# Third weight sum on VectorE, the FFN inputs in another order and other buffers, and the down projection's residual added by DMA

## Chip, core and metric

The kernel runs on one NeuronCore of a Trainium2 chip. The metric is the device time of one execution in microseconds (us): 2263.05 us before the change, the median of three runs (2258.35 to 2268.36). Times inside the execution come from one profiled run of 2262.26 us, whose span from the first to the last instruction is 2260.6 us. TensorE's matmul queue is PE, VectorE is DVE, ScalarE is ACT, GpSimd is POOL and SyncE's DMA queue is SP.

## What is computed

One layer of a hybrid decoder runs over 512 prompt tokens and 8 sample tokens, 520 columns in all. Everything is in 32-bit floats, and the kernel keeps activations transposed: features on the partitions, tokens along the row.

```python
def mixer(xn, ...):
    proj = xn @ w_in                                  # 2048 x 6160
    ...
    out = jnp.concatenate([ya, yb], axis=-1) @ w_out  # 2048 x 2048
    return out, conv_new, s_new

def conv_ffn(xn, prev, w_up, conv_w, conv_b, w_down):
    u, v = jnp.split(xn @ w_up, 2, axis=-1)           # 2048 x 11264
    cu, new = causal_dwconv(u, prev, conv_w)
    h = jax.nn.silu(cu + conv_b) * v
    return h @ w_down, new                            # 5632 x 2048

def trunk(x, ...):
    m, c_new, s_new = mixer(rmsnorm(x, norm_mix_g[l]), ...)
    x = x + m
    f, f_new = conv_ffn(rmsnorm(x, norm_ffn_g[l]), ...)
    x = x + f
    return rmsnorm(x, final_norm_g), ...
```

## The kernel before

**Stages.** The kernel runs the input projection with the gated convolution and the linear attention (to 683 us), the mixer's output projection `wo` (683 to 880 us), the up projection with the convolution gate (880 to 1778 us), the down projection (1778 to about 2190 us) and the end with the final norm. Every matmul is a 128x128 weight tile against 260 columns. A product of full precision takes three of them: weights and activations are split into a rounded part (`hi`, `xh`) and the rest (`lo`, `xl`), and hi·xh, hi·xl and lo·xh are summed.

**Seven products.** The last three projections multiply 2x2 block matrices by seven block products instead of eight (Winograd's form of Strassen's scheme). The seven products of a group run in the order `ORDER` = 1, 5, 6, 2, 7, 3, 4; each has 24 matmuls. Their weights are four blocks, `raw[1,1]`, `raw[1,2]`, `raw[2,1]`, `raw[2,2]`, of 128x1024 numbers (512 KB each), and sums of them: a tile `s` holds first raw[2,2]+raw[2,1] (product 5), then that plus raw[1,1] (product 6), then that plus raw[1,2] (product 3), and raw[2,1] takes raw[1,1] on top (product 7). `weights` (L1016) loads the blocks and says who forms each sum: VectorE by an entry of `sums`, or an accumulating DMA of GpSimd by an entry of `dma`. The third sum is a DMA in the second chunk of `wo` (`dma3`) and VectorE's elsewhere; the seventh is VectorE's in the very first group and a DMA in all others.

**Groups.** `wo` has two chunks `c` of the contraction with four groups `g` each, `up` has 44 groups, `down` five chunks of four groups. The main loop (L1403 to L1479) walks through all products `i`. At product 0 of a group it issues three of the next group's weight loads (`begin`), at product 2 the fourth (`load_rest`), and two products ahead `prepare` makes `hi` on ACT and `lo` on DVE and forms the next sum. After each call `in_order` ties the instructions of every engine and of both DMA queues to the order of the program, so an instruction that waits holds up all that follow on its engine or queue.

**Results of wo and down.** `chunk_finish` (L1256) copies the partial sums in PSUM to other banks (ACT, L1269) and adds the finished ones onto `acc[g, q]`, four SBUF tiles of 128x520 per group (DVE, `onto`, L1263). `load_residual` (L1216) fills these tiles with the residual by POOL's queue before the first chunk adds to them: x for `wo`, and x1 (x plus the mixer's result) for `down`.

**Inputs of the FFN.** In the second chunk of `wo`, `projected(g)` (L1302) turns `acc` into the inputs of the up projection, in steps numbered by products since the group's first one; a step of 7 or more falls into the next group. `ready(q)` stores `acc[g, q]` to DRAM as x1 (L1308, SP) and scales it into `xg[q]` (ACT, L1311). `square(q)` squares `acc` on ACT into a tile `fh` and adds that by DMA (POOL) to the norm's sum `ssq`, whose second half is the tile `R`. `sub`, `minus` and `split` form the seven inputs, "forms" 1 to 7. Forms 2 and 3 are written over the `acc` tiles. Forms 5, 4 and 6 have no home yet in the first three groups: `out` splits them into a fresh tile and the source and stores both to `t_d` in DRAM (L1331, SP), and `load_sum` (L1367) loads them back during the last group. Fresh tiles come from `tmp()`, a rotation of eight 128x520 tiles named `t`; a tile is given out again when all that reads it is done, a store to DRAM included.

**The gate.** `gate(t)` (L1148) multiplies the up projection's two halves `z` and `v` by `R`, runs the convolution and forms h. For t < 2 the factor `R` comes late, and z is multiplied as a whole there.

## Time and profile before

| | |
|---|---|
| median of three runs | 2263.05 us (2258.35 to 2268.36) |
| profiled execution | 2262.26 us |
| its span | 2260.6 us |
| mean granted TensorE clock | 0.986 of 2.4 GHz |
| busy ACT, POOL | 1039.6 us (46%), 461.4 us (20%) |
| DMA | 419.10 MB, mean 185 GB/s |
| chain that ended last | PE 88%, DMA 6%, DVE 3% |

A row of the timeline gives start, duration, engine, line, operation and tiles, and in brackets how long the engine had been idle before it and what ended that. A releaser is the instruction whose end came last among those waited for. Where the granted clock reads below 1.00 over a stretch, TensorE ran at 1.2 GHz for part of it.

### The profile page before, as it was taken

The page shows a single profiled execution, that of the slowest core. Times are in us where ns is not written, and L with a number is a line of the kernel's source. Part 1 is how long each engine was busy: PE and PEld are TensorE (multiplying, and loading weights), DVE is VectorE, ACT ScalarE, POOL GpSimd, SP SyncE. Part 2 cuts the span into 40 slices and gives each one's busy share as a digit, 9 for nine tenths or more (in the row PEclk, how much of TensorE's full clock was granted, in tenths as well). Part 3 has the DMA queues.
Part 4 walks back from the last instruction along what each step waited for, and adds up shares of the span by engine and source line. Part 5 has one row for each costly group of instructions (what it writes and reads, how often), then busy time and mean ns, then how long its engine had stood idle before and what let it go on. Part 6 is the DMA issues. An engine that isn't in the chain of part 4 may idle for free.

```text
span 2260.6 us, 43939 instructions
## 1 busy us (share of the span) xinstructions
PE 2195.8 (97%) x17963; PEld 2172.9 (96%) x17963; DVE 1631.3 (72%) x2188; ACT 1039.6 (46%) x1486; POOL 461.4 (20%) x640
## 2 busy tenths in 40 slices
PE   8999999999999977999999999999999999999997
PEld 7998999999999977999999999999999999999997
DVE  5345364444448676888989889889898777778776
ACT  5334434322334465555555555555555444444445
POOL 3023132221323311121221222113121500000100
PEclk9999999999999989999999999999999999999999
DMA  8343354374787789476676766667666987876944
GB/s 249 84 126 105 107 156 113 87 210 121 201 248 242 219 233 299 126 195 174 167 195 160 194 173 178 183 160 193 174 180 191 308 236 218 258 205 195 282 122 151
DMA packets 459751, 419.10 MB, mean 185 GB/s; under 512 B 21353, under 2 KB 413445, under 8 KB 459405
## 3 DMA queue, kind: packets, MB, share of 16 engines
q1 hardware_dynamic: 418353, 285.89, 43.7%
q0 software_dynamic: 39872, 128.17, 21.7%
q8 instruction: 141, 2.31, 0.4%
q10 hardware_dynamic: 1324, 2.23, 0.3%
q14 instruction: 61, 0.50, 0.1%
HBM read 294.13 MB, written 79.25 MB: 165 GB/s over the span
## 4 chain that ended last, share of the span: by engine, by line
PE 88%; DMA 6%; DVE 3%; ACT 1%; POOL 1%; issue 1%; SPq 0%; ACTq 0%; DVEq 0%; POOLq 0%
PE mm L1108 27%; PE mm L134 25%; PE ms L1108 11%; PE y L1249 8%; PE x L1249 8%; PE f L1249 3%; PE e L1249 3%; PE ms L830 1%; DMA t_d<-t 1%; DMA form<-g_d 1%; DMA x_d<-acc 1%; DVE lo L1087 1%; DMA raw<-in_w_down_dram 0%; DMA acc<-x_d 0%; PE ms L1516 0%
## 5 line engine op out<-in xcount | busy, mean ns | idle before, releaser
L1083 ACT ACTIVATE hi<-raw 128x1024 fp32r<-128x1024 f32 x288 | 304.4, 1057 | 225.7 <-issue 79.5
L1108 PE MATMUL mm<-yh,hi 128*128 128x260 f32 x1408 | 398.6, 283 | 2.8 <-ACT ms L1118 2.4
L1108 PE MATMUL mm<-yl,hi 128*128 128x260 f32 x1408 | 397.8, 283 | 0.0
L1108 PE MATMUL mm<-yh,lo 128*128 128x260 f32 x1408 | 397.5, 282 | 0.0
L1087 DVE TENSOR_TENSOR lo<-raw,hi 128x1024 fp32r<-128x1024 f32 x288 | 351.3, 1220 | 57.7 <-ACT hi L1083 57.6
L1087 DVE TENSOR_TENSOR lo<-s,hi 128x1024 fp32r<-128x1024 f32 x216 | 265.3, 1228 | 111.0 <-ACT hi L1083 105.6
L1083 ACT ACTIVATE hi<-s 128x1024 fp32r<-128x1024 f32 x216 | 228.4, 1057 | 223.9 <-DVE s L1032 92.6
L1108 PEld LDWEIGHTS mm<-yh,hi 128*128 128x128 f32 x1408 | 265.1, 188 | 3.3 <-ACT ms L1118 2.6
L1108 PEld LDWEIGHTS mm<-yl,hi 128*128 128x128 f32 x1408 | 265.9, 189 | 0.0
L1108 PEld LDWEIGHTS mm<-yh,lo 128*128 128x128 f32 x1408 | 265.8, 189 | 0.1
L1108 PE MATMUL ms<-b,hi 128*128 128x260 f32 x1408 | 256.6, 282 | 4.6 <-DVE b L118 4.6
L106 DVE TENSOR_TENSOR lo<-raw,hi 128x1024 fp32r<-128x1024 f32 x112 | 144.4, 1290 | 138.1 <-ACT hi L105 131.5
L105 ACT ACTIVATE hi<-raw 128x1024 fp32r<-128x1024 f32 x112 | 118.0, 1055 | 265.3 <-PE mm L134 226.2
L1108 PEld LDWEIGHTS ms<-b,hi 128*128 128x128 f32 x1408 | 217.1, 188 | 4.8 <-DVE b L118 4.8
L1249 PE MATMUL y<-form,hi 128*128 128x260 f32 x1120 | 210.7, 288 | 11.2 <-ACT f L1269 11.2
L1249 PE MATMUL x<-form,hi 128*128 128x260 f32 x1120 | 208.4, 286 | 9.2 <-ACT f L1269 7.4
L1036 POOL DMA_DIRECT2D raw<-raw x71 | 63.5, 895 | 700.1 <-DVE s L1032 585.2
L1108 PE MATMUL ms<-b,lo 128*128 128x260 f32 x704 | 198.5, 282 | 0.0
L1249 PEld LDWEIGHTS y<-form,hi 128*128 128x128 f32 x1120 | 177.6, 193 | 11.6 <-ACT f L1269 11.6
L1249 PEld LDWEIGHTS x<-form,hi 128*128 128x128 f32 x1120 | 175.5, 191 | 10.0 <-ACT f L1269 7.6
L1032 DVE TENSOR_TENSOR s<-s,raw 128x1024 f32<-128x1024 f32 x140 | 170.9, 1221 | 2.5
L1249 PE MATMUL y<-form,lo 128*128 128x260 f32 x560 | 161.3, 288 | 3.8 <-DVE lo L1087 3.8
(324 smaller groups left out, 5563.1 us busy)
## 6 DMA issues: line engine op xcount, KB each, us to landing
raw<-in_w_up_dram SPq DMA_DIRECT2D x176, 512.0 KB
raw<-in_w_down_dram SPq DMA_DIRECT2D x96, 512.0 KB
raw<-in_w_in_dram SPq DMA_DIRECT2D x92, 512.0 KB
raw<-raw POOLq DMA_DIRECT2D x71, 512.0 KB, 5.9
form<-f_d SPq DMA_DIRECT2D x126, 260.0 KB
f_d<-t POOLq DMA_DIRECT2D x80, 260.0 KB, 5.3
raw<-in_w_out_dram SPq DMA_DIRECT2D x32, 512.0 KB
form<-g_d POOLq DMA_DIRECT2D x56, 260.0 KB, 7.9
```

The costliest lines, as they stand in the source:

```text
L105: nc.scalar.activation(hi, raw, AF.Copy)
L106: nc.vector.tensor_tensor(lo, raw, hi.bitcast(F32), op=ALU.subtract)
L134: nc.tensor.matmul(o, w, xx, start=first and i == 0, stop=last and i == 2)
L830: nc.tensor.matmul(pb[:, c * 64 : (c + 1) * 64], L[:, c, :], rhs[:, c], start=True, stop=True,)
L1032: return lambda: nc.vector.tensor_tensor(out, x, y, op=ALU.add)
L1036: return lambda: nc.gpsimd.dma_start(out, x, accum_op=ALU.add)
L1083: nc.scalar.activation(his[i], src, AF.Copy)
L1087: nc.vector.tensor_tensor(los[i], src, his[i].bitcast(F32), op=ALU.subtract)
L1108: nc.tensor.matmul(st["bank"][b], w[:, k, :], x, start=b not in st["used"] and k == 0 and j == 0, stop=k == 7 and j == 2, skip_group_check ...
L1249: nc.tensor.matmul(ps[:, m, :], w[:, k, m * P : (m + 1) * P], x, start=b not in st["used"] and k == 0 and j == 0, stop=k == 3 and j == 2, ...
```

## The change

Five edits, in the order of the diff:

- **Weight sums.** The third sum is always VectorE's. The seventh is a DMA for `up` and for all chunks but the first of `wo` and `down`; in both first chunks VectorE forms it.
- **Gate.** For t < 2, z is multiplied by R first and v three products later; for other t, v as before.
- **Residual of down.** `load_residual` serves `wo` alone. In `down`, the first chunk writes its first result onto `acc` instead of adding it (ACT, with the sign as scale; four of six), and during the second chunk `add_residual` adds x1 by accumulating DMAs of POOL's queue, four per group, for the group two further on.
- **Stores of x1.** In the last group of `wo`, tiles 1 and 2 of `acc` are copied into a fresh tile (ACT) and stored from there.
- **Order of the FFN's inputs.** Form 2 is split one product earlier, t4 is written over `xg[2]` instead of a fresh tile, form 7 is split half a product later, and form 6 is stored one product later, at 10.5.

```diff
@@ -1013,7 +1013,7 @@
-    def weights(source, dma3):
+    def weights(source, dma7):
@@ -1038,17 +1038,15 @@
         }
-        sums = {5: plus(s, raw[2, 2], raw[2, 1]), 6: plus(s, s, raw[1, 1])}
-        dma = {}
-        if state:
-            dma[7] = dma_plus(raw[2, 1], raw[1, 1])
-        else:
+        sums = {
+            5: plus(s, raw[2, 2], raw[2, 1]), 6: plus(s, s, raw[1, 1]), 3: plus(s, s, raw[1, 2]),
+        }
+        if not dma7:
             sums[7] = plus(raw[2, 1], raw[2, 1], raw[1, 1])
-        if dma3:
-            dma[3] = dma_plus(s, raw[1, 2])
-        else:
-            sums[3] = plus(s, s, raw[1, 2])
-        return dict(src=src, sums=sums, dma=dma, bank={}, used=set(), rest=loads[3])
+        return dict(
+            src=src, sums=sums, bank={}, used=set(), rest=loads[3],
+            seventh=dma_plus(raw[2, 1], raw[1, 1]) if dma7 else lambda: None,
+        )
@@ -1060,7 +1058,8 @@
         kind, at = groups[n]
-        state[kind, at] = weights(source(kind, at), kind == "wo" and at[0] == 1)
+        state[kind, at] = weights(source(kind, at), kind == "up" or at[0] > 0)
@@ -1152,10 +1151,9 @@
         yield d
-        nc.vector.tensor_tensor(v[:, :T], v[:, :T], R, op=ALU.mult)
+        x = z[:, 2 : 2 + T] if t < 2 else v[:, :T]
+        nc.vector.tensor_tensor(x, x, R, op=ALU.mult)
         yield d + 0.5
-        if t < 2:
-            nc.vector.tensor_tensor(z[:, 2 : 2 + T], z[:, 2 : 2 + T], R, op=ALU.mult)
         c = tmp()
@@ -1166,6 +1164,9 @@
         )
+        if t < 2:
+            yield d + 3
+            nc.vector.tensor_tensor(v[:, :T], v[:, :T], R, op=ALU.mult)
         yield d + 3.5
@@ -1213,12 +1214,21 @@
-    def load_residual(kind, g):
+    def new_sums(g):
         for q in range(4):
...
+    def load_residual(g):
+        new_sums(g)
+        for q in range(4):
+            nc.gpsimd.dma_start(two(acc[g, q]), rows_of(xT_d, "wo", g, q))
+    def add_residual(g):
+        for q in range(4):
             nc.gpsimd.dma_start(
-                two(acc[g, q]), rows_of(xT_d if kind == "wo" else x1_d, kind, g, q)
+                two(acc[g, q]), rows_of(x1_d, "down", g, q), accum_op=ALU.add
             )
@@ -1260,7 +1270,11 @@
             a = two(acc[g, q])
-            nc.vector.tensor_tensor(a, a, inner(bk[b]), op=op)
+            if kind == "down" and c == 0 and (q, b) not in ((1, "f"), (3, "a")):
+                scale = 1.0 if op == ALU.add else -1.0
+                nc.scalar.activation(a, inner(bk[b]), AF.Copy, scale=scale)
+            else:
+                nc.vector.tensor_tensor(a, a, inner(bk[b]), op=op)
@@ -1305,7 +1319,12 @@
             a, m = acc[g, q], first_tile("wo", g, q // 2)
-            nc.sync.dma_start(rows_of(x1_d, "wo", g, q), two(a))
+            kept = a
+            if g == NG - 1 and q in (1, 2):
+                kept = tmp()[:, :T]
+                nc.scalar.activation(kept, a, AF.Copy)
+            nc.sync.dma_start(rows_of(x1_d, "wo", g, q), two(kept))
             xg[q] = tmp()[:, :T]
@@ -1347,20 +1366,20 @@
         yield 8
-        t4 = tmp()[:, :T]
+        split(xg[2], *form(2, g))
+        t4 = xg[2]
         minus(t4, t2, xg[2])
...
         out(4, t2)
-        out(7, t4)
         yield 9
         square(1)
-        split(xg[2], *form(2, g))
+        out(7, t4)
+        yield 10
         t3 = xg[1]
         sub(t3, xg[3], xg[1])
-        yield 9.5
-        out(6, t3)
         yield 10.5
         square(2)
+        out(6, t3)
         yield 11
@@ -1396,7 +1415,7 @@
     load_rest(0)
-    load_residual("wo", 0)
+    load_residual(0)
     prepare(0)
@@ -1433,10 +1452,8 @@
         prepare(i + 2)
-        if j == 0 and 3 in state[kind, at]["dma"]:
-            state[kind, at]["dma"][3]()
         if j == 5 and more:
-            state[groups[n + 1]]["dma"][7]()
+            state[groups[n + 1]]["seventh"]()
         run_steps(i + 0.5)
@@ -1448,7 +1465,7 @@
             if c == 0 and j == 4 and g + 1 < NG:
-                load_residual("wo", g + 1)
+                load_residual(g + 1)
             if c == 0 and g == NG - 1 and j >= 1:
@@ -1461,14 +1478,14 @@
                 load_form("down", 0, x)
-            if j == 5:
-                load_residual("down", 0)
         if kind == "down":
...
                 drain()
-            if c == 0 and j == 4 and g + 1 < NG:
-                load_residual("down", g + 1)
+            if c == 0 and j == 0:
+                new_sums(g)
+            if c == 1 and j == 5:
+                add_residual((g + 2) % NG)
             if c + 1 < NCD:
...
                     load_form("down", c + 1, 0)
```

On ACT, this is the stretch of group 2 of `wo`'s second chunk in which the forms of group 1 are written (names: `e`, `f`, `x` PSUM tiles; `hi` the rounded weights; `b` form 2 or 3 in an `acc` tile; `yh` form 7; `t` from `tmp()`). Before:

```order
L1269 ACTIVATE e<-x 128x2x260
L1083 ACTIVATE hi<-raw 128x1024
L117 ACTIVATE t<-t 128x520
L117 ACTIVATE yh_9171<-t 128x520
L1320 ACTIVATE fh<-acc 128x520
L117 ACTIVATE b_9203<-t 128x520
L1083 ACTIVATE hi<-raw 128x1024
L117 ACTIVATE t<-t 128x520
L1269 ACTIVATE f<-x 128x2x260
L1083 ACTIVATE hi<-s 128x1024
```

and of the change, from the same copy of `e` on:

```order
L1283 ACTIVATE e<-x 128x2x260
L117 ACTIVATE b_9158<-t 128x520
L1082 ACTIVATE hi<-raw 128x1024
L117 ACTIVATE t<-t 128x520
L1339 ACTIVATE fh<-acc 128x520
L117 ACTIVATE yh_9200<-t 128x520
L1082 ACTIVATE hi<-raw 128x1024
L1283 ACTIVATE f<-x 128x2x260
L1082 ACTIVATE hi<-s 128x1024
L1339 ACTIVATE fh<-acc 128x520
L117 ACTIVATE t<-t 128x520
```

The second split into `t` (form 6) moved from ahead of the copy of `f` to three instructions behind it, and form 2 (`b_9203`, now `b_9158`) to directly behind the copy of `e`.

On DVE, the changed program has in the same stretch one sum more (`s<-s,raw`, the third):

```order
L118 TENSOR_TENSOR b_9159<-t,b_9158 128x520
L583 SCALAR_TENSOR_TENSOR t<-t 128x520
L1086 TENSOR_TENSOR lo<-raw,hi 128x1024
L118 TENSOR_TENSOR t<-t 128x520
L118 TENSOR_TENSOR yl_9201<-t,yh_9200 128x520
L1032 TENSOR_TENSOR s<-s,raw 128x1024
L1086 TENSOR_TENSOR lo<-raw,hi 128x1024
L1277 TENSOR_TENSOR acc<-acc,y 128x520 x2
```

It stands directly ahead of the `lo` of product 7's weights; before, GpSimd issued a DMA `s<-raw` for it.

On POOL's queue, the changed program's second chunk of `down` reads (each `raw<-raw` is a seventh sum, each `acc<-x_d` a lot of four residual tiles):

```order
L1036 DMA raw<-raw 128x1024 x2
L1230 DMA acc<-x_d 128x2x260 x4
L1036 DMA raw<-raw 128x1024
L1230 DMA acc<-x_d 128x2x260 x4
L1036 DMA raw<-raw 128x1024
L1230 DMA acc<-x_d 128x2x260 x4
L1036 DMA raw<-raw 128x1024
L1230 DMA acc<-x_d 128x2x260 x4
```

The lots of four stood before in the first chunk, as plain loads, with the seventh sums of that chunk between them.

## Rows read from the trace of the kernel before

**Rows 1.** The page's first part: busy time, share, instructions.

```profile
PE 2195.8 (97%) x17963; PEld 2172.9 (96%) x17963; DVE 1631.3 (72%) x2188; ACT 1039.6 (46%) x1486; POOL 461.4 (20%) x640
```

**Rows 2.** PE's timeline, waits between 780 and 940 us and in down.

```profile
782.94 0.80 PE L1249 MATMUL f<-form,hi 128*128 128x260 f32 x2 [3.52 <-ACT hi L1083]
...
838.82 0.80 PE L1249 MATMUL x<-form,hi 128*128 128x260 f32 x2 [7.37 <-ACT f L1269]
...
901.94 0.39 PE L1108 MATMUL ms<-b,hi 128*128 128x260 f32 x1 [4.64 <-DVE b L118]
...
937.85 0.39 PE L1108 MATMUL mm<-yh,hi 128*128 128x260 f32 x1 [2.43 <-ACT ms L1118]
...
1804.37 0.58 PE L1249 MATMUL y<-form,lo 128*128 128x260 f32 x1 [3.81 <-DVE lo L1087]
```

**Rows 3.** Windows: from:to, us; busy PE, PEld, DVE, ACT, POOL; clock; DMA share; GB/s.

```profile
744.59:764.83 20.24, 20.24 (x171) 20.24 (x170) 15.78 (x17) 8.42 (x9) 13.40 (x19) 1.00 0.89 286
764.83:792.24 27.41, 23.43 (x170) 22.92 (x169) 15.06 (x17) 12.58 (x18) 6.37 (x9) 0.88 0.68 195
792.24:819.76 27.52, 22.45 (x171) 22.24 (x170) 20.90 (x27) 17.59 (x28) 4.33 (x6) 0.88 0.87 234
819.76:850.00 30.24, 22.87 (x171) 22.66 (x170) 21.03 (x27) 17.38 (x28) 5.28 (x7) 0.83 0.88 229
850.00:879.92 29.92, 22.29 (x171) 21.90 (x169) 22.36 (x29) 18.34 (x29) 5.68 (x7) 0.89 1.08 307
879.92:907.44 27.52, 22.51 (x173) 22.03 (x173) 17.52 (x22) 12.97 (x21) 2.79 (x4) 0.94 1.12 295
907.44:929.33 21.89, 21.89 (x178) 21.66 (x177) 13.41 (x13) 13.35 (x19) 6.88 (x5) 1.00 0.45 120
929.33:952.30 22.97, 20.54 (x171) 20.26 (x169) 20.97 (x29) 12.79 (x18) 0.86 (x1) 1.00 0.51 127
784.80:892.00 107.20, 87.13 (x650) 86.32 (x650) 81.03 (x100) 68.54 (x111) 17.23 (x20) 0.87 0.93 253
```

**Rows 4.** ACT's timeline: the waits behind the first two of rows 2.

```profile
781.83 1.06 ACT L1083 ACTIVATE hi<-s 128x1024 fp32r<-128x1024 f32 x1 [7.45 <-DMA s<-raw]
...
837.64 0.64 ACT L117 ACTIVATE t<-t 128x520 fp32r<-128x520 f32 x1 [10.08 <-DMA t_d<-t]
```

**Rows 5.** The chain of waits in order of time: start, us, what.

```profile
826.60 11.57 DMA t_d<-t
...
877.18 10.85 DMA x_d<-acc
...
894.03 7.06 DMA x_d<-acc
```

**Rows 6.** DVE's timeline: the waits behind the third and the last of rows 2.

```profile
901.18 0.70 DVE L118 TENSOR_TENSOR b<-t,b 128x520 fp32r<-128x520 f32 x1 [7.74 <-DMA x_d<-acc]
...
1801.96 1.23 DVE L1032 TENSOR_TENSOR s<-raw 128x1024 f32<-128x1024 f32 x1 [6.70 <-DMA raw<-in_w_down_dram]
```

**Rows 7.** Groups of instructions by form, DVE and ACT, 792.24 to 850.00 us.

```profile
L1032 DVE TENSOR_TENSOR s<-s,raw 128x1024 f32<-128x1024 f32 x3 | 3.7, 1225 | 0.1
...
L1263 DVE TENSOR_TENSOR acc<-acc,x 128x520 f32<-128x520 f32 x4 | 2.7, 690 | 0.1
...
L1269 ACT ACTIVATE f<-y 128x520 f32<-128x520 f32 x1 | 0.6, 586 | 0.0
```

**Rows 8.** DMA queues, 1906.9 to 1927.2 us, one group of down: packets, MB, share.

```profile
q1 hardware_dynamic: 2112, 2.10, 33.5%
q0 software_dynamic: 150, 0.55, 14.3%
```

**Rows 9.** Windows of down, columns as in rows 3.

```profile
1778.46:1827.06 48.60, 44.22 (x342) 43.84 (x342) 33.65 (x39) 19.08 (x23) 19.90 (x31) 0.93 1.00 313
1827.06:1867.52 40.46, 40.46 (x338) 40.46 (x337) 31.54 (x33) 16.83 (x18) 2.10 (x3) 1.00 0.79 233
1906.90:1927.20 20.30, 20.30 (x171) 20.30 (x170) 15.86 (x17) 8.41 (x9) 0.86 (x1) 1.00 0.48 131
1947.50:1967.70 20.20, 20.20 (x170) 20.20 (x170) 15.75 (x17) 8.42 (x9) 0.86 (x1) 1.00 1.08 329
```

## The prediction

> **What bounds the kernel now.** I read the page's first part, then the waits of PE in its timeline, then windows over the groups in which they lie, and last the engine or DMA behind each wait. TensorE's matmul queue is busy 97% of the span [rows 1], and the change leaves the number of matmuls alone. So it can give or cost only what PE loses in waits, and in the slow clock behind them.
>
> The losses near the change lie in two places. The first runs from the second chunk of `wo` into the third group of `up`. A group without a wait takes 20.24 us, the first row [rows 3]; the seven that follow take 27.41, 27.52, 30.24, 29.92, 27.52, 21.89 and 22.97 us, together 187.47. Seven times 20.24 is 141.68, and two pairs of small matmuls for the norm add about 1.6. **44.2 us** are lost. The waits of PE make up 31.5 of them: 3.5 for product 3 of the first group, three of one kind (7.37 stands in the rows, 5.07 and 6.10 are its like), 4.64, 2.43, and four small ones of 2.4 together [rows 2]. The other 12.7 us are matmuls at 1.2 GHz behind a wait: the granted clock is 0.83 to 0.89 in the groups of the chunk, 1.00 in the one ahead [rows 3].
>
> The second place is the start of `down`: its first two groups take 48.60 us, the next two 40.46 [rows 9]. Less 0.8 us of marker matmuls and a transpose, **7.3 us** are lost, 3.81 of them in one wait [rows 2].
>
> The causes, wait by wait. (A) Product 3 waits for ACT's `hi<-s`, and that for the third sum by DMA [rows 4]. (B) Three times ACT stands 8 to 10 us before a split into a fresh `t` because the tile's last content is still on its way to `t_d` [rows 4, 5]; the copy of `f`, for which PE waits, stands behind it. PE loses 7.37 us where ACT waits 10.08, so ACT has a lead of 2.7 us. (F) The split of form 3 over `acc` waits 7.74 us on DVE for the store of x1 [rows 5, 6]. (G) The first gates delay a copy of ACT by 2.43 us. (H) In `down`, DVE's sum waits 6.70 us for weights [rows 6] while the DMA engines are full: share 1.00 over the whole stretch [rows 9].
>
> **The change part by part.** Profiled run 2262.26 us, span 2260.6.
>
> *Third sum by VectorE.* (A) goes. DVE pays 1.22 us in each of four groups [rows 7]. It is busy 20.9 us in a group of 20.24 already, by the third row [rows 3], so from the second group on it would be about 1.9 us too long, 5.6 us over three groups; with the lead of 2.7, 2.9 us could reach PE. The busy figure counts overlapping ends of instructions, so nothing may reach it. Bounds 0 and 5.6; I take 1.5, because part runs beside the DMA wait below.
>
> *Seventh sum by VectorE in the first chunks.* Seven more sums at 1.22 us. DVE has 15.8 of 20.2 us to do there [rows 3, 9], so they cost nothing; without that cover it would be 1.22 per group.
>
> *Order and homes of the inputs.* Before, a group takes nine fresh tiles out of a rotation of eight, and form 6 gets the tile from which form 5 was stored two products (5.8 us) earlier; the store spends 11.57 us on the chain alone [rows 5]. Now eight are taken. Form 5's tile is next wanted four products later (11.6 us), form 6's three (8.7 us). With the lead of 2.7 us that covers 11 to 14 us, and form 6's `hi` is now behind the copy of `f`. (B) goes in the first groups. What is late next is the DMA system itself. From 784.8 to 892 us, between the first store of x1 and the last loads of form 6, its share is 0.93: 99.7 us of work, by the last row [rows 3]. The queue of accumulating DMAs worked 14.3% of 20.3 us for one sum [rows 8], 2.9 us; three third sums fall in this stretch, which leaves 91.0 us. Full windows read up to 1.12, the sixth row [rows 3], so that work takes 81 to 91 us. Without waits the first store comes at 778, some 4 us of work are done by 785, and the rest ends between 863 and 872. Product 7 of the first `up` group wants form 6 at 764.8 + 4 x 20.24 + 4 x 2.9 + 1.4 = 859. So 4 to 13 us of wait come back there or just ahead; I take 9. A wait of that size brings slow clock: eight waits brought 12.7 us now, so some 1.6 each, and I add 2.5. Bounds: 0 (sums of squares share these engines and may land later) and 17.
>
> *Copies ahead of the store.* (F) goes for 2 x 0.62 us of ACT, which is busy 13 of 27.5 us there [rows 3]. The split of form 2 comes a product earlier and wants the x1 store of tile 3 in 2.5 products (7.2 us); such a store took 10.85 us at the fullest point [rows 5]. That wait lies ahead of the one for form 6 and inside it, so it adds nothing to the sum.
>
> *Gate.* z first, v later: (G), 2.43 us and its clock, is inside the 44.2.
>
> *Down.* The DMA engines lose before 1800 us two lots of residual (8 x 0.85 us, from 6.8 us for 2.10 MB in rows 8) and one seventh sum, 9.7 us; the late weights were 6.7 late. (H) goes; about 1 us stays of two waits of 0.5 that other things cause. ACT gains 16 copies of 0.586 us in place of DVE's 0.690 [rows 7], 2.3 us per group on 8.4 of 20.3 [rows 9]: nothing.
>
> *Residual added in the second chunk.* Sixteen DMAs; half a sum of 512 KB is 1.5 us, so 5.9 us per lot, 23.5 in all. In the middle groups the engines are half empty (0.48), where chunks meet they are full (1.08) [rows 9], and two of four lots end up there. PE waits nowhere in that stretch, and weights are requested a group ahead. Bounds 0 and 2 x 5.9; I take 0, as in the groups where they are full now and nothing waits.
>
> **Sum.** 44.2 + 7.3 = 51.5 us to be had; 9 + 2.5 + 1.5 + 1 = 14.0 stay. 2262.26 - 37.5 = 2224.8; the median lies 0.8 above the profiled run, so **2225.6 us**.
>
> **Rivals.**
>
> *The wait moves to form 2 (0.20).* With DMA still full in groups two to four, DVE stands before `b` of form 2 until tile 3's x1 has landed: 10.85 against 7.2 us plus the lead of 2.7, 1 to 4 us each, with clock 2 us more, and DVE's own 5.6 us come on top. Some 13 us more stay: 2239. For it: rows 5. Against it: DMA shares of 0.68 to 0.88 in the first three groups, and 2.9 us less work in each.
>
> *All is recovered (0.13).* If DMA takes the 81 us or less, only the 1 us in `down` stays: about 2212.
>
> *The added residual delays weights (0.10).* If the accumulating DMAs are served beside the loads that were asked for earlier, each of two lots at a chunk's end holds them up by 5.9 us, less the lead 3.2, twice, and 1 us of clock: 2233. No wait in [rows 9] shows it; there was no second stream of this size there. The Trainium skill ("DMA: Bandwidth & Descriptors", section "Queues, rings and completion order") says that each DMA engine takes turns between the queues that have work for it, a packet at a time. By that rule the time would be this one; first come, first served would give 2225.6.
>
> *Slower: the DMA engines are the bound (0.04).* If their work, not its order, sets the second chunk's time, the 44.2 us stay under other names, and the 23.5 us of adds come through in full where chunks meet; less 7.3 that is 2279. It decides from a share of 1 in every group of the chunk, and from no slack in weights a group ahead. Against it: 0.68, 0.87 and 0.88 in three groups [rows 3] and 0.48 in `down`. The same page's section "Issuing engines are not separate DMA queues" says that all queues share the same 16 engines. By it the residual costs DMA time wherever it is put; the shares decide whether anyone waits.
>
> That the change doesn't do what it says is no rival: the order of the instructions shows every part.
>
> **Numbers.** Forecast 0.48 (2217 to 2232); the rivals as above; 0.05 for a gain under 0.5%. About 0.5% (11 us) is what a measurement of this kernel can tell from no change. The range runs from all recovered with 3 us for the spread of runs, 2209, to the form 2 case with its upper price and the adds, 2247. Faster 0.90, same 0.06, slower 0.04.
>
> **What would show it.** In the changed profile PE's waits for ACT's copy of `f` are gone, DMA s<-raw is no releaser, and groups one to three of the chunk take 20.2 to 22 us. The fourth, or the first of `up`, is several us too long, with a load from `t_d` or an x1 store behind the wait, at a DMA share above 1. The start of `down` is 6 to 7 us shorter, and no wait on a DMA shows in its second and third chunk. It is wrong if groups of the chunk stay above 25 us, if DVE sets PE's pace there, or if `raw` is waited for where chunks of `down` meet.

## The result, and the profile after

The changed kernel takes **2235.38 us** (median of 4 runs, 2233.18 to 2237.94), the kernel before in the same session 2262.62 us (4 runs, 2258.35 to 2268.36). The ratio is 0.9878, with a 95% interval of 0.9853 to 0.9904. Forecast were 2225.6 us and a range of 2209 to 2247. The sign and the range hold; the time came out 9.8 us longer, and outside the 2217 to 2232 us that had the highest chance (0.48).

The two profiled executions have spans of 2260.6 and 2236.2 us. Their difference of 24.4 us splits at five points of PE's timeline:

| stretch | before | after | difference | forecast |
|---|---|---|---|---|
| start to the first matmul of `wo` (not edited) | 683.35 | 685.43 | +2.1 | 0 |
| second chunk of `wo` and three groups of `up` | 187.47 | 162.55 | -24.9 | -31.2 |
| first two groups of `down` | 48.60 | 41.14 | -7.5 | -6.3 |
| second group of `down`'s third chunk | 20.23 | 24.74 | +4.5 | 0 |
| all else | | | +1.4 | 0 |

PE is busy for 98% of the shorter span (97% in [rows 1]), by the first line of the page:

```profile
PE 2189.3 (98%) x17963; PEld 2165.8 (97%) x17963; DVE 1634.4 (73%) x2183; ACT 1049.2 (47%) x1504; POOL 459.6 (21%) x629
```

The first line of the table is no effect: over fourteen kernels with the same code there it lay between 681.7 and 686.8 us. Inside the second line the chunk's four groups, 27.41, 27.52, 30.24 and 29.92 us in [rows 3], have become shorter; the first group of `up` has grown from 27.52 to 30.97. The windows of the changed kernel by group (us, busy time of PE, PEld, DVE, ACT and POOL, granted clock, DMA share, GB/s), the last the third group of `up`:

```profile
766.91:787.14 20.23, 20.23 (x171) 20.23 (x169) 16.40 (x18) 12.72 (x18) 4.41 (x6) 1.00 0.83 251
787.14:807.83 20.69, 20.46 (x171) 20.28 (x169) 20.62 (x27) 16.23 (x26) 3.39 (x4) 1.00 0.95 269
807.83:829.91 22.08, 20.72 (x170) 20.40 (x169) 21.98 (x28) 17.46 (x29) 3.67 (x6) 1.00 1.05 281
829.91:856.46 26.55, 22.39 (x171) 21.94 (x169) 25.04 (x31) 19.99 (x33) 5.72 (x7) 0.94 1.08 290
856.46:887.43 30.97, 25.78 (x172) 24.44 (x173) 17.96 (x22) 13.71 (x22) 2.54 (x3) 0.83 1.08 298
...
909.34:929.46 20.12, 20.12 (x170) 20.12 (x169) 19.50 (x27) 11.91 (x17) 0.85 (x1) 1.00 0.56 141
```

Against 20.24 us, and 1.6 for the norm's matmuls, 19.3 us are lost where 44.2 were lost before. DVE is busy for 20.62 of 20.69 and 21.98 of 22.08 us in the second and third row, and for 25.04 of 26.55 in the fourth. PE's waits there, from its timeline of the changed kernel (what answers to [rows 2]):

```profile
826.95 0.48 PE L1259 MATMUL x<-form,hi 128*128 128x260 f32 x2 [1.36 <-DVE acc L1277]
850.58 0.48 PE L1259 MATMUL y<-form,hi 128*128 128x260 f32 x2 [2.92 <-DVE acc L1277]
856.46 0.36 PE L1107 MATMUL mm<-bh,hi 128*128 128x260 f32 x1 [1.25 <-DVE acc L1277]
863.89 0.39 PE L1107 MATMUL mm<-yl,hi 128*128 128x260 f32 x1 [0.83 <-DMA yl<-t_d]
865.63 0.38 PE L1107 MATMUL mm<-yh,hi 128*128 128x260 f32 x1 [0.87 <-DMA yh<-t_d]
...
872.46 0.59 PE L1107 MATMUL mm<-yl,hi 128*128 128x260 f32 x1 [2.42 <-DVE yl L118]
```

The waits for ACT's `f`, for `hi<-s` and for the gate are gone. In their place stand waits for DVE's addition to `acc` (it frees the PSUM bank), small ones for loads from `t_d`, and one for DVE's `yl`. DVE makes that `yl` right behind the split of form 2, the step which the change had moved a product earlier, and there it stands 9.21 us for the x1 store, as its timeline and the chain of waits say:

```profile
869.23 0.70 DVE L118 TENSOR_TENSOR b<-t,b 128x520 fp32r<-128x520 f32 x1 [9.21 <-DMA x_d<-acc]
```

```profile
851.40 7.57 DMA t_d<-t
...
858.99 0.02 SPq L1327
...
859.03 10.10 DMA x_d<-acc
```

The chain shows two delays, one behind the other: SP issues the store of x1 only when a store to `t_d` has landed, and the x1 store then needs 10.10 us. SP does not wait for that data. The `t_d` store of 851.40 is the eighth DMA ahead of the x1 store on SP. By the semaphores that the trace records, this program gives SP's DMAs eight in turn (687 of SP's 715 DMAs take the one that the eighth ahead of them had), and each waits until its own is free. The windows of 5 us show the price in clock: 0.50, TensorE's lower level of 1.2 GHz, just behind the waits.

```profile
865.00:870.00 5.00, 3.30 (x13) 2.43 (x13) 0.74 (x2) 2.71 (x5) 0.00 (x0) 0.84 1.06 394
870.00:875.00 5.00, 2.58 (x12) 2.54 (x12) 5.00 (x6) 2.83 (x5) 0.85 (x1) 0.50 1.13 328
```

In `down`, windows by group: the two first groups, then the last of the second chunk and the two first of the third (what answers to [rows 9]):

```profile
1755.63:1776.53 20.90, 20.90 (x173) 20.90 (x174) 16.95 (x21) 12.04 (x17) 6.31 (x12) 1.00 1.08 357
1776.53:1796.77 20.24, 20.24 (x171) 20.24 (x170) 14.39 (x14) 10.49 (x13) 0.00 (x0) 1.00 0.50 155
...
1897.90:1918.12 20.22, 20.22 (x170) 20.22 (x169) 15.78 (x17) 8.41 (x9) 5.76 (x8) 1.00 1.11 282
1918.12:1938.37 20.25, 20.25 (x171) 20.25 (x169) 11.26 (x12) 7.36 (x8) 2.56 (x3) 1.00 1.13 285
1938.37:1963.11 24.74, 20.71 (x170) 20.32 (x169) 20.34 (x21) 9.38 (x10) 1.74 (x2) 1.00 0.85 246
```

The wait at the start is gone. A new one stands where the third chunk has just begun: PE for DVE's `lo`, DVE's sum for `raw`:

```profile
1942.00 0.39 PE L1259 MATMUL y<-form,lo 128*128 128x260 f32 x1 [3.23 <-DVE lo L1086]
```

```profile
1939.59 1.23 DVE L1032 TENSOR_TENSOR s<-raw 128x1024 f32<-128x1024 f32 x1 [6.12 <-DMA raw<-in_w_down_dram]
```

### The profile page after: what moved, and what is told of

Its sections match the earlier page's. It is cut to its first block, busy times and chain, and to the rows that moved or that the text cites. A ratio compares the mean times of both kernels' runs of the same rounds, so it can differ in the third digit from the quotient of the medians.

```text
span 2236.2 us, 43928 instructions
## 1 busy us (share of the span) xinstructions
PE 2189.3 (98%) x17963; PEld 2165.8 (97%) x17963; DVE 1634.4 (73%) x2183; ACT 1049.2 (47%) x1504; POOL 459.6 (21%) x629
## 4 chain that ended last, share of the span: by engine, by line
PE 84%; DMA 2%; DVE 2%; issue 1%; ACT 1%; SPq 0%; ACTq 0%; DVEq 0%
PE mm L1107 28%; PE mm L134 20%; PE ms L1107 11%; PE x L1259 8%; PE y L1259 8%; PE e L1259 3%; PE f L1259 3%; DMA raw<-in_w_down_dram 1%; PE ms L830 1%; DVE lo L1086 0%; DMA t_d<-t 0%; DVE s L1032 0%; DMA x_d<-acc 0%; PE ms L1533 0%; DMA raw<-in_w_out_dram 0%
## 5 line engine op out<-in xcount | busy, mean ns | idle before, releaser
L1036 POOL DMA_DIRECT2D raw<-raw x64 | 57.2, 894 | 651.0 <-DVE s L1032 481.6
L1032 DVE TENSOR_TENSOR s<-s,raw 128x1024 f32<-128x1024 f32 x144 | 176.0, 1222 | 2.5
L134 PE MATMUL mm<-xh,hi 128*128 128x260 f32 x768 | 160.7, 291 | 3.8 <-ACT xh L120 3.8
```

What stands on the lines that cost most here:

```text
L134: nc.tensor.matmul(o, w, xx, start=first and i == 0, stop=last and i == 2)
L1032: return lambda: nc.vector.tensor_tensor(out, x, y, op=ALU.add)
L1036: return lambda: nc.gpsimd.dma_start(out, x, accum_op=ALU.add)
```

## The experiments

Three stretches tell the parts apart in every run: S, the four groups of `wo`'s second chunk and the first three of `up` (where an expectation names a stretch "from the chunk's second group", it is this one, by its numbers); D, the first two groups of `down`; M, the second group of `down`'s third chunk. All from PE's timelines, in us; ratios are to the kernel before on the same chip.

| kernel | S | D | M | median | ratio (95%) |
|---|---|---|---|---|---|
| before | 187.47 | 48.60 | 20.23 | | 1 |
| changed | 162.55 | 41.14 | 24.74 | 2235.38 | 0.9878 (0.9853 to 0.9904) |
| third_alone | 171.30 | 48.61 | 20.23 | 2248.59 | 0.9940 (0.9925 to 0.9955) |
| third_by_dma | 174.58 | 41.14 | 25.46 | 2248.01 | 0.9939 (0.9924 to 0.9954) |
| residual_loaded | 161.08 | 42.61 | 20.23 | 2229.16 | 0.9853 (0.9836 to 0.9870) |
| residual_middle | 159.71 | 41.14 | 20.23 | 2228.95 | 0.9853 (0.9838 to 0.9869) |
| subs_by_pool | 166.49 | 41.14 | 27.02 | 2241.62 | 0.9914 (0.9899 to 0.9929) |
| all_kept | 160.45 | 41.13 | 25.05 | 2234.75 | 0.9880 (0.9863 to 0.9896) |
| store_by_pool | 157.99 | 41.15 | 26.48 | 2233.17 | 0.9874 (0.9859 to 0.9889) |
| down_seventh_dma | 160.29 | 41.14 | 25.16 | 2235.43 (one run) | |
| third_left_out | 158.63 | 41.14 | 25.25 | 2232.38 | 0.9873 (0.9847 to 0.9899) |
| gate_and_copies_undone | 165.04 | 41.14 | 25.54 | 2238.14 | 0.9901 (0.9878 to 0.9923) |
| stores_middle | 158.07 | 41.14 | 20.23 | 2227.53 | 0.9850 (0.9829 to 0.9871) |
| stores_middle_td | 159.25 | 41.14 | 20.23 | 2226.33 | 0.9846 (0.9825 to 0.9868) |

Four kernels have S unedited (changed, residual_loaded, residual_middle, down_seventh_dma): 159.7 to 162.6, mean 160.9. A difference in S of 2 us from one profile is therefore little; the changed kernel's own profile is the slowest of the four.

### third_alone: the kernel before with one edit

```diff
-        state[kind, at] = weights(source(kind, at), kind == "wo" and at[0] == 1)
+        state[kind, at] = weights(source(kind, at), False)
```

> The kernel before with one edit: in the second chunk of wo the third sum is made by DVE instead of an accumulating DMA. Theory (order and homes of the FFN's inputs made most of the gain): PE's wait for hi<-s of product 3 goes (3.5 us and its slow clock, some 5 us together), the waits of ACT for the stores to t_d stay, and DVE, which waits in that chunk anyway, hides its 1.2 us per group. From the chunk's second group to the third group of up about 182 us (187.5 before, 162.6 changed), the whole some 2257 us. Rival (the accumulating DMAs were what filled the DMA engines): the stores come early enough as well, the stretch falls under 170 us, the whole to about 2245.

Measured: S 171.30, 16.2 us less than before, where the theory had some 5 and the rival over 17. The rival is nearly right. ACT's waits for stores to `t_d` did not stay as they were, they became shorter; two of its three, from its timeline, against 10.08 us in [rows 4]:

```profile
826.64 0.64 ACT L117 ACTIVATE t<-t 128x520 fp32r<-128x520 f32 x1 [6.64 <-DMA t_d<-t]
852.19 0.64 ACT L117 ACTIVATE t<-t 128x520 fp32r<-128x520 f32 x1 [5.97 <-DMA t_d<-t]
```

PE's waits for `f` fell with them, from 5.07, 7.37 and 6.10 us to 1.37, 5.20 and 3.55. So the edit helped the stores too, not only product 3. That it did so by taking 512 KB per group off the accumulating queue is the likely reason, but no run isolates it. D is 48.61 as before: this edit does nothing there.

### third_by_dma: the changed kernel without that edit

```diff
+        third = lambda: None
+        if dma3:
+            del sums[3]
+            third = dma_plus(s, raw[1, 2])
...
         prepare(i + 2)
+        if j == 0:
+            state[kind, at]["third"]()
```

> The changed kernel with the third sum of the second chunk of wo given back to an accumulating DMA, all else kept. Theory (DVE too full costs about 4 us there, the DMA engines about as much): PE's wait for hi<-s of some 3.5 us comes back once with its slow clock, three sums of 2.9 us of all DMA engines lengthen the full stretch, DVE's 1.2 us per group go: the stretch takes about 168 us instead of 162.6, the whole some 2241 us (2237 to 2248). Rival (DVE's 21 to 22 us per group are the bound of the second and third group): those groups return to 20.3 us and the whole is no slower than the changed kernel, 2231 to 2236.

Measured: S 174.58, 12.0 us above the changed kernel, twice the theory's 5 to 6. The rival (no slower) is refuted: all four groups of the chunk are 24 to 27.5 us long. The theory let the wait for `hi<-s` come back once, as it stands in [rows 2]. It came back in every group, and one for `lo<-s` behind each:

```profile
781.39 0.80 PE L1264 MATMUL f<-form,hi 128*128 128x260 f32 x2 [2.91 <-ACT hi L1087]
...
805.98 0.51 PE L1264 MATMUL f<-form,hi 128*128 128x260 f32 x2 [0.87 <-ACT hi L1087]
...
831.16 0.51 PE L1264 MATMUL f<-form,hi 128*128 128x260 f32 x2 [2.01 <-ACT hi L1087]
832.42 0.59 PE L1264 MATMUL f<-form,lo 128*128 128x260 f32 x1 [0.75 <-DVE lo L1091]
...
854.94 0.51 PE L1264 MATMUL f<-form,hi 128*128 128x260 f32 x2 [0.61 <-ACT hi L1087]
```

Eight such waits make 9.1 us, and the granted clock is 0.87 to 0.93 in the first three groups. In the kernel before, a longer wait for `f` at the product just ahead, in all but the first group, had given the third sum the time to arrive: one cause hid the other. The four kernels give a table of two edits. The third sum by DVE is worth 16.2 us alone and 12.0 beside the new order; the new order and homes (with the gate and the copies) 12.9 us alone and 8.7 beside it.

### residual_loaded and residual_middle: the residual of `down`

The first undoes the residual's edit:

```diff
-            if kind == "down" and c == 0 and (q, b) not in ((1, "f"), (3, "a")):
+            if False and (q, b) not in ((1, "f"), (3, "a")):
...
+            if j == 5:
+                load_residual(0, "down")
...
-            if c == 0 and j == 0:
-                new_sums(g)
-            if c == 1 and j == 5:
-                add_residual((g + 2) % NG)
+            if c == 0 and j == 4 and g + 1 < NG:
+                load_residual(g + 1, "down")
```

> The changed kernel with the residual of the down projection handled as before: loaded into the sums ahead of and in the first chunk, the first results added by DVE, nothing added in the second chunk. Theory 1 (the early residual loads made the wait at the start of down, the late adds the new wait where the second chunk meets the third): the first two groups of down take 45 to 48 us instead of 41.1, the second group of the third chunk 20.3 instead of 24.7; the whole 2234 to 2238 us. Theory 2 (the seventh sum by DVE cured the start of down): the first two groups stay at 41 us and the other gain comes too, about 2231 us.

The second keeps it and moves the four lots:

```diff
-            if c == 1 and j == 5:
-                add_residual((g + 2) % NG)
+            lot = {(1, 0, 5): 2, (1, 1, 5): 3, (2, 1, 5): 0, (2, 2, 1): 1}.get((c, g, j))
+            if lot is not None:
+                add_residual(lot)
```

> The changed kernel with the four lots of accumulating DMAs for the residual moved: two in the first two groups of the second chunk, two in the middle groups of the third, none while the next chunk's inputs are loaded. Theory (the lots hold up weights where the DMA engines are full): the second group of the third chunk takes 20.3 us instead of 24.7, no window of down there has a DMA share above 1.08, the whole is about 4.5 us faster than the changed kernel, 2231 us. Rival (the lots cost the same wherever they are, or the wait there comes from the input loads): the wait for raw moves to another group or stays, 2235 us.

Measured: M is whole again in both, 20.23 us. With the loads back, D is 42.61 us, not 45 to 48: theory 2 is much nearer. As it was placed, the residual's edit brought 1.5 us in D and cost 4.5 in M. Both kernels reach a ratio of 0.9853.

How the lots hold up the weights is seen on SP's queue (start, us it took to issue, count). In the changed kernel:

```profile
1903.67 23.82 SPq L612 DMA_DIRECT2D form<-f_d  x20
1927.60 4.57 SPq L1029 DMA_DIRECT2D raw<-in_w_down_dram  x3
```

The last four of these twenty loads, issued beside the second lot, alone:

```profile
1918.43 9.06 SPq L612 DMA_DIRECT2D form<-f_d  x4
```

In residual_middle, whose third chunk begins at 1913.73:

```profile
1898.83 14.35 SPq L612 DMA_DIRECT2D form<-f_d  x20
1913.62 4.74 SPq L1029 DMA_DIRECT2D raw<-in_w_down_dram  x3
```

With two lots beside them SP needs 1.19 us on average for each load of the next chunk's inputs, and 2.27 for the last four; without lots it needs 0.72 (14.35 us for 20). SP's pace follows the transfers: from 1918.43 to 1927.50 the lots' queue took 73.6% of the DMA engines and SP's moved 1.01 MB; in the 9.8 us ahead, with no lot under way, SP's had moved 3.50 MB. The weights stand behind these loads in SP's program: they are asked for 9.5 us into the third chunk (1918.12), where they are asked for as it begins in the other kernel. In the middle of a chunk no such loads are there. Then a lot costs nothing, even at a DMA share of 1.14, as the window of residual_middle's third chunk with a lot in it shows:

```profile
1954.21:1974.44 20.23, 20.23 (x170) 20.23 (x169) 15.78 (x17) 8.41 (x9) 8.26 (x8) 1.00 1.14 224
```

### down_seventh_dma: the other half of the start of `down`

```diff
-        state[kind, at] = weights(source(kind, at), kind == "up" or at[0] > 0)
+        state[kind, at] = weights(source(kind, at), kind != "wo" or at[0] > 0)
```

> The changed kernel with the seventh sum in the first chunk of down given back to the accumulating DMA; the residual is still added late. Theory 1 (the wait at the start of down was the total of DMA work, of which the residual's loads were 6.8 us and the sum 2.9): the first two groups take 41 to 43 us, against 41.1 in the changed kernel, 42.6 with loaded residual and a seventh sum by DVE, and 48.6 before. Theory 2 (the accumulating DMA itself made the wait, whatever the load beside it): 46 to 48 us.

Measured: D 41.14 us, theory 1. Of the two loads on the DMA engines at that place, residual and seventh sum, either one removed all or nearly all of the wait (41.14 and 42.61); only together do they make 48.6. So neither edit "caused" the 7.5 us: the wait appears once their sum is more than the queue can hide.

### subs_by_pool: three instructions per group off DVE

```diff
-        sub(t1, xg[0], xg[1])
-        minus(t2, t1, xg[3])
+        nc.gpsimd.tensor_tensor(t2, xg[1], xg[0], op=ALU.subtract)
+        nc.gpsimd.tensor_tensor(t1, xg[0], xg[1], op=ALU.subtract)
+        nc.gpsimd.tensor_tensor(t2, t2, xg[3], op=ALU.subtract)
...
-        sub(t3, xg[3], xg[1])
+        nc.gpsimd.tensor_tensor(t3, xg[3], xg[1], op=ALU.subtract)
```

> The changed kernel with four of the small sums per group of wo's second chunk (for the FFN's forms 4, 5 and 6) made by POOL, which takes three instructions of 0.61 us off DVE's 21.7 us per group. Theory (DVE sets PE's pace in the chunk's second to fourth group, 162.6 us for the stretch): DVE needs 19.9 us, the second and third group go from 20.69 and 22.08 to 20.3 us, PE's waits for DVE's acc go, the stretch falls by 4 to 6 us, the whole to about 2230 us. Rival 1 (the DMA engines bound the end of the stretch): the groups go to 20.3 as well, but the fourth group or the first of up grows by as much, the whole stays at 2235. Rival 2 (POOL is slow or slows DVE down): the splits of forms 5 and 6 wait for POOL, the stretch grows.

Measured: S 166.49, rival 2. POOL's instructions take 1.3 to 2.2 us where DVE's took 0.70, and DVE's next ones are held up by them. POOL's timeline, then DVE's, at the same time:

```profile
785.20 1.47 POOL L1363 TENSOR_TENSOR t<-t 128x520 f32<-128x520 f32 x1 [1.29 <-ACT t L1330]
786.75 2.18 POOL L1364 TENSOR_TENSOR t<-t 128x520 f32<-128x520 f32 x1
788.89 1.30 POOL L1365 TENSOR_TENSOR t<-t 128x520 f32<-128x520 f32 x1
```

```profile
785.51 2.24 DVE L1032 TENSOR_TENSOR s<-s,raw 128x1024 f32<-128x1024 f32 x1
787.68 0.68 DVE L1277 TENSOR_TENSOR acc<-acc,x 128x520 f32<-128x520 f32 x1
788.94 2.34 DVE L1086 TENSOR_TENSOR lo<-s,hi 128x1024 fp32r<-128x1024 f32 x1 [0.58 <-ACT hi L1082]
```

The sum of two SBUF tiles takes 2.24 us and ends 1.1 us after POOL's first instruction; `lo` takes 2.34 and ends 1.1 us after POOL's third. Without POOL both take 1.22. The addition of a PSUM bank to `acc` runs in 0.68 us while POOL works. The Trainium skill ("SBUF — State Buffer", section "SBUF: two separate sides") states this: a port pair is shared between VectorE and GpSimd, whoever has it keeps it for the whole instruction, and an operation of VectorE with two SBUF inputs wants it. These rows agree. So this run does not tell what DVE's load costs; third_left_out does.

### all_kept and store_by_pool: the store ahead of form 2

```diff
 all_kept:
-            if g == NG - 1 and q in (1, 2):
+            if g == NG - 1:
 store_by_pool:
-            nc.sync.dma_start(rows_of(x1_d, "wo", g, q), two(kept))
+            eng = nc.gpsimd if g == NG - 1 else nc.sync
+            eng.dma_start(rows_of(x1_d, "wo", g, q), two(kept))
```

> The changed kernel where in the last group of wo's second chunk all four results are copied by ACT ahead of their store, not two, so that the split of form 2 over acc waits for no store. Theory (that store, in the queue behind the loads from t_d, sets the 9.2 us wait of DVE and so the end of the stretch): DVE's wait for x_d<-acc there goes, PE's waits for yl fall to those on t_d, the first group of up takes 26 us or less instead of 31, the whole is about 5 us faster, 2230 us. Rival (the loads from t_d land no earlier and are wanted next): the wait moves to them, no more than 1 us is won. A second rival: the copies take two more tiles of the rotation of eight, and a later user of such a tile waits for the same store.

> The changed kernel where in the last group of wo's second chunk the four x1 stores are issued on POOL's queue and not behind the loads from t_d on SP's. Theory (the store of tile 3 is late because it stands behind some 4 MB of loads in its own queue): from issue to landing it takes 2 to 5 us instead of 10, DVE's wait of 9.2 us at the split of form 2 falls below 4, the first group of up takes about 27 us instead of 31, the whole is some 4 us faster, 2231 us. Rival (it is late because all 16 engines are full, whatever the queue): it lands as late, and the time stays at 2235.

Measured: all_kept has S 160.45, no gain: its second rival. The wait did not go, it moved to ACT, which wants a tile of the rotation whose copy is not yet stored, and PE waits 5.53 us at one place instead. ACT's timeline:

```profile
864.18 0.91 ACT L1330 ACTIVATE t<-acc,par 128x260 f32<-128x260 f32 x2 [8.03 <-DMA x_d<-t]
```

store_by_pool has S 157.99, some 3 us less than the mean of the four unedited ones (stores_middle, with the same edit, has 158.07), and no wait for an x1 store at the end. But the reason is not the one expected. By the view of `x_d` there, issue to landing still takes this long:

```profile
DMA to landing us min/median/max: 6.7/9.3/10.3
```

What changed is the issue: POOL issues the two stores from `acc` at 844.6 and 849.3, 16 and 21 us after the fourth group's start at 828.28; SP had issued them at 855.87 and 859.03, 26 and 29 us after 829.91. They no longer stand in SP's program among the loads from `t_d`, each of which waits for the eighth DMA ahead of it, mostly such a load too. SP's waits in the changed kernel from 840 to 870 us (total us, times, longest):

```profile
SPq L1388 <- DMA yh<-t_d: 4.1, 3, 2.4
SPq L1388 <- DMA yl<-t_d: 3.0, 4, 1.6
```

So theory and rival share this one: the place in the issuing engine's program was the lever, the transfer is as slow on either queue. In the median (ratio 0.9874) the gain is hardly visible; M is 26.48 us in this run.

And most of the loss at this place stays without that wait. The first group of `up` still takes 27.98 us, begins with a wait for DVE's `acc`, and is slow behind it:

```profile
853.28 0.56 PE L1107 MATMUL mm<-bh,hi 128*128 128x260 f32 x1 [2.76 <-DVE acc L1277]
```

```profile
853.27:881.25 27.98, 26.21 (x172) 25.17 (x173) 17.10 (x21) 13.33 (x22) 3.35 (x5) 0.83 1.10 316
```

### third_left_out: what DVE's load costs

```diff
+        if dma3:
+            del sums[3]
```

> The changed kernel without the third sum in the second chunk of wo: neither DVE nor a DMA makes it, so product 3 there multiplies the sum of product 6 (part of the computation is left out). DVE has 20.5 us of work per group instead of 21.7, the DMA engines have what they have in the changed kernel. Theory (DVE sets PE's pace in the second to fourth group): these groups lose 1 us instead of 7 to 9, PE's waits for acc are gone, the stretch from the chunk's second group to the third group of up takes 155 to 158 us, against 159.7 to 162.6 in four runs that have it unchanged. Rival (full DMA engines bound the end): the first of up grows by what the groups ahead gain, 160 us or more.

Measured: S 158.63. The second and third group are whole, the fourth and the first of `up` hardly change:

```profile
786.85:807.07 20.22, 20.22 (x171) 20.22 (x170) 20.15 (x26) 16.88 (x28) 3.44 (x4) 1.00 1.01 282
807.07:827.40 20.33, 20.33 (x171) 20.27 (x169) 20.00 (x26) 16.46 (x27) 3.42 (x4) 1.00 1.05 281
827.40:852.65 25.25, 20.86 (x171) 20.32 (x169) 24.23 (x30) 20.28 (x34) 5.97 (x7) 1.00 1.10 308
852.65:883.22 30.57, 26.28 (x172) 24.91 (x173) 17.96 (x22) 13.72 (x22) 2.54 (x3) 0.83 1.12 310
```

The third sum on DVE costs 2.2 us in these two groups, shown by 20.69 and 22.08 becoming 20.22 and 20.33. The theory's "lose 1 us instead of 7 to 9" is wrong for the fourth group: there 30 DVE instructions fall into one group even without the third sum, and PE's two waits for `acc` stay, 1.14 us in the group and 2.75 at the change from `wo` to `up`, against 2.92 and 1.25 in the changed kernel. That part is only read from the trace.

### gate_and_copies_undone

```diff
-        x = z[:, 2 : 2 + T] if t < 2 else v[:, :T]
-        nc.vector.tensor_tensor(x, x, R, op=ALU.mult)
+        nc.vector.tensor_tensor(v[:, :T], v[:, :T], R, op=ALU.mult)
         yield d + 0.5
+        if t < 2:
+            nc.vector.tensor_tensor(z[:, 2 : 2 + T], z[:, 2 : 2 + T], R, op=ALU.mult)
...
-            if g == NG - 1 and q in (1, 2):
+            if False:
```

> The changed kernel with two small parts undone: no copies ahead of the x1 stores of the last group, and the first two gates multiply v by R ahead of z. Theory: the split of form 3 over acc waits for the store again (7.7 us of DVE before), PE loses 3 to 5 us at the first group of up, and 2.4 us at its second or third group while a copy of ACT stands behind the gate; with slow clock the stretch takes 167 to 171 us, the whole about 2242. Rival (the wait at form 2, a product earlier, covers the one at form 3): only the 2.4 us of the gate come back, 163 to 165 us.

Measured: S 165.04, the rival. PE waits for the gate again, and the third group of `up` takes 24.53 us instead of 20.12:

```profile
913.69 0.39 PE L1107 MATMUL mm<-yh,hi 128*128 128x260 f32 x1 [2.44 <-ACT ms L1117]
```

So the gate's order is worth 4.4 us, 2.44 of wait and the rest slow clock. Without the copies DVE does wait 3.65 us at form 3, but the first group of `up` takes 30.60 us, as with them (30.97): the wait at form 2 covers it, and the copies bring nothing here.

### stores_middle and stores_middle_td: towards a better version

Both have the diffs of residual_middle and store_by_pool; the second also this one:

```diff
+                eng = nc.gpsimd if g == NG - 2 else nc.sync
...
-                    nc.sync.dma_start(d, x)
+                    eng.dma_start(d, x)
```

> The changed kernel with both edits that gained alone: the residual's lots in the middle groups of down's second and third chunk, and the x1 stores of wo's last group on POOL's queue. They lie 1000 us apart, so the gains add: 4.5 to 5.5 us where down's chunks meet, about 3 us at the end of the stretch (158 us). The whole 7 to 8 us below the changed kernel, 2227 us, a ratio of 0.9845 to before. Rival (the late t_d stores set the end of the stretch whatever the x1 stores do): 2230.

> As the run with both edits, and the stores to t_d of wo's third group go on POOL's queue too, since with the x1 stores on POOL ACT stood 5.5 us for a tile whose store to t_d was on its way. Theory: that wait goes, the first group of up takes 25 us instead of 28, the whole is 2 to 3 us below the run with both edits. Rival (POOL's queue gets late: its sums of squares, the seventh sum of the next weights and these stores go out one after another, 0.85 us each): the seventh product of the fourth group or of the first of up waits, the time is the same or longer.

Measured: 2227.53 us, ratio 0.9850 (the theory had 2227), and 2226.33 us, ratio 0.9846. Both beat the kernel before, and the changed one by 6 to 7 us, reckoned from the ratios; the intervals overlap a little. They are not told apart from each other nor from residual_middle (0.9853). What every profile shows is the gain from moving the lots, M at 20.23 us. With the `t_d` stores on POOL too, ACT's wait for a tile (4.0 us in stores_middle) is gone, but S is 159.25. That is the rival's time, not its mechanism: PE waits for no seventh sum there, but again for `acc` (2.77 and 1.23 us) and for loads from `t_d`.

## Why the prediction was right, and where it was wrong

**The bound, and what was to be had.** Right: 44.2 and 7.3 us were the places, and the gain came from there and nowhere else. All five causes were gone or changed in the way described. Their sizes were not additive, though. (A) was put at 3.52 us; the third sum's move proved worth 12 to 16 us (third_by_dma, third_alone), because the wait was hidden behind (B) in three groups, and, as third_alone suggests, because its DMAs made (B) longer. The sum took all of 44.2 as one and so did not suffer. PE's timeline has nine waits there (three small ones, not four); at 12.7 / 9 = 1.4 us of slow clock each instead of 1.6 the sum stays as it is.

**What stays in the chunk.** Forecast 13 us (9 + 2.5 + 1.5), measured 19.3, or 17.6 on average over the four kernels with that code. The DVE term was of the right size: 1.5 forecast, 2.2 shown by third_left_out. The step that failed is "What is late next is the DMA system itself" with 9 us for the load of form 6: the loads from `t_d` cost PE only 2.8 us in five small waits. In their place the runs show two things. One is a chain in the last group: SP's program holds back the x1 store, DVE stands before form 2 for it (9.21 us), and PE pays 2.42 us and slow clock. store_by_pool, which takes this wait out, gains some 3 us. The prediction had written that the wait at form 2 "lies ahead of the one for form 6 and inside it, so it adds nothing". It lies behind the loads of the forms ahead, and PE pays for it: the first rival's mechanism, in one group of four, at far less than its 13 us. The other is DVE at the end of `wo`, where PE waits 2.92 and 1.25 us for `acc`: DVE is busy for 25.04 of 26.55 us there, and stands 0.88 us for another x1 store. These waits stay in store_by_pool and in third_left_out, and so does the slow clock of the first group of `up` (0.83). With store_by_pool the last group of `wo` and the first of `up` still lose some 12 us (24.99 and 27.98 against 20.24 each). How these split among DVE, the loads and the clock no run shows. A volume of bytes over a rate gave nearly the right sum for another reason; that was luck.

**Copies ahead of the store.** "(F) goes for 2 x 0.62 us": PE's wait at form 3 went, but by cover, not by the copies; undoing them brought DVE's wait back (3.65 us) and cost PE nothing measurable.

**Gate.** Right, and worth 2.9 us with its clock in the kernel before (22.97 us in [rows 3] against 20.12), 4.4 in gate_and_copies_undone.

**Down.** Right, 7.5 us against 6.3. The reason given, 9.7 us less DMA work against weights 6.7 late, was a threshold; the runs show that either part alone suffices for nearly all of it.

**Residual added in the second chunk.** Wrong: taken at 0 with bounds of 0 and 11.8, measured 4.5 us in the profiled run and 4.5 to 6.8 in all eight kernels that keep the lots there. The failing premise is "weights are requested a group ahead". They are, when SP is free; with two lots beside its loads it is not. The third rival, put at 0.10, was the one that happened, at one of its two places. Its lead of 3.2 us stands in none of the rows, and its terms add up to 2232 when the clock is counted once; neither bears on the sum. It drew on the Trainium skill's rule that an engine takes turns between queues by packets ("DMA: Bandwidth & Descriptors", section "Queues, rings and completion order"). The trace agrees with it: from 1918.43 to 1927.50 both queues moved at once, 1030 packets of SP's and 795 of the lots', and the loads slowed from 0.72 to 1.19 us each on average. The windows [rows 9] could not show it, since no second stream of this size was there before; a share of 1.08 without a wait was taken as proof that the share alone does no harm.

**The sum.** Of the 9.8 us, 4.5 are the lots and 4.6 to 6.3 what stays in the chunk, less 1.2 more gained at the start of `down`; the rest is within what unedited stretches differ by from run to run. "DMA engines are the bound" (0.04) did not come: with a share of 1.05 the third group lost 1.84 us, and DVE was the cause.

## What to carry to other kernels

Where several waits stand in one group, a cause that shows 3 us can be worth 12 once the others are gone: find out by undoing one part at a time in the final version. Before adding DMAs to a second queue, look at what else is being loaded then, and at which weights stand behind it in the issuing engine's program: the price came as a late request both times here. In `down` the loads ahead of the weights had been slowed; in `wo` the store stood among DMAs that waited for one another. A store that other engines must wait for should not be issued behind loads that wait themselves.

## What the runs showed of the hardware

An accumulating DMA costs the engines more per byte than a load. In the changed kernel from 1918.12 to 1942.00 the queues shared the 16 engines like this (packets, MB, share):

```profile
q1 hardware_dynamic: 5482, 5.41, 72.6%
q0 software_dynamic: 1232, 1.59, 39.0%
```

That is 5.9 us of all engines per MB added (0.390 x 23.88 / 1.59) against 3.2 per MB loaded (0.726 x 23.88 / 5.41). Both are estimates, since the shares add up to more than 1. With half-empty engines [rows 8] gives much the same, 5.3 (0.143 x 20.3 / 0.55) and 3.2. Plain loads on POOL's own queue, from 700 to 730 us of the changed kernel, took 2.9 (4.23 MB at a share of 40.4%), so it is the adding that costs, not the queue.

Beside a POOL instruction on SBUF tiles, DVE took 2.24 and 2.34 us instead of 1.22 when it read two SBUF tiles, and its usual 0.68 when one operand was in PSUM. POOL's 2.18 us, against 1.30 to 1.47 for its neighbours, would fit its having waited for DVE's sum in turn, which ended at 787.75; no run tests that. And a store of 260 KB took 7 to 11 us to land while the engines were full, on either queue (6.7 to 10.3 us by the view of `x_d` in store_by_pool, 7.06 and 10.85 in [rows 5]).
